# Lower parts of three slices and two weights moved behind the SSM mixer, and the last block's residual added by TensorE ahead of the mixer and at the end

## The chip, the cores and the metric

The program runs on one core of a Trainium2 chip. The core has a matrix engine (TensorE, PE in the profile), three engines for elementwise work (VectorE or DVE, ScalarE or ACT, GpSimd or POOL), and a queue engine (SyncE, SP) that does nothing here but issue transfers. Each engine runs its own instructions in a fixed order and waits for others by semaphores. The order is written into the program by a list scheduler that simulates the program beforehand; `self.order(x, y)` in the source only tells it to put x behind y. The metric is the device time of one execution in microseconds (us). Lower is better.

## What is computed

One inference step of a two-layer streaming encoder, for 1024 prompt positions and 64 sample positions with 1024 channels, in 32-bit floats. Layer 0 mixes tokens with banded attention, layer 1 with a complex diagonal state space model (S5). Around each mixer, and around the gated convolutional FFN behind it, stand two RMS norms and a residual:

```
h = x + rms_norm(mixer(rms_norm(x, g_pre_mix)),  g_post_mix)
x = h + rms_norm(conv_ffn(rms_norm(h, g_pre_ffn)), g_post_ffn)

rms_norm(x, g) = x * rsqrt(mean(x * x) + eps) * g

# mixer B, per group of 16 channels and complex state of 64
state[t] = lambda * state[t-1] + B u[t];   y = Re(C state) + D u
z = gelu(y);  ag = z @ w_glu + b_glu;  out = ag[:1024] * sigmoid(ag[1024:])

# conv_ffn
up = h @ w_up;  c = causal depthwise conv of width 3;  y = (gelu(c_a) * c_b) @ w_down
```

## The kernel before

**Layout.** Activations lie with channels on the 128 partitions: eight slices of 128 channels, and positions along the free axis. Positions are cut into three blocks of 384, 384 and 320 (blocks 0, 1 and 2; block 2 is "the last block" here). Two slices together are called a pair below, so a block has pairs 0 to 3.

**Products.** Large products are made from split operands. Each operand is the sum of an upper part, rounded to a format that TensorE takes at full rate (`h`, as in `zh`, `whl[:, 0]`), and a lower part, the rest (`l`). A product is three matmuls (`mm3`, L222): upper weight with lower activation, upper with upper, lower weight with upper activation. The upper part is copied by ScalarE and the lower part is a subtraction on VectorE. For weights this is `split_unit` (L214, timed at L217): a unit of 128x1024 is loaded into one of two `raw` buffers and split into `whl`. Plain 32-bit matmuls, as those with the identity, are made by TensorE in two recorded instructions each.

**From the first FFN to the mixer.** `ffn` ends with block 2's down projection (`down`, L637). `post_norm` (L312) then takes the statistics (`rstd`, L238: squares on ScalarE, sums on VectorE, a matmul with a column of ones at L267, a root at L271, three small VectorE operations, a transpose at L285 that brings the factor into PSUM as `pr`). In `apply`, VectorE multiplies each pair by `pr` (L329), and the residual `xs` (tiles `xl`, loaded long before) is added at L332. For block 2 behind the first FFN all four additions are VectorE's; at the program's end pairs 0 and 2 are GpSimd's and pairs 1 and 3 VectorE's, and each pair is stored at once (L336).

`ssm_norm` (L1154) takes the mixer's own statistics of the result. Meanwhile TensorE runs `fill` matmuls (L228, timed at L231), which compute nothing that is used: eight ahead of the statistics and one behind them. The factor goes through `ex` (L1181) and a matmul (L1182) into `rs` (L1184, L1185), by which the mixer's input is scaled. In parallel `ssm_bounce` (L1120) copies each pair into tiles `xs` in another order (L1140, ScalarE) and SP writes them to `hd` in DRAM (L1146); `ssm_load` (L1187) reads them back as `U` with channels and time rearranged, one quarter (two slices) at a time in two halves.

**The mixer** (`ssm`, L1205) runs 32 pairs of groups in batches of one or two. A batch loads its parameters (`pm`, five tiles ahead, L1222), multiplies into PSUM (L1258), and goes through VectorE: two products with cosine and sine tables (L1289, L1294), an addition (L1295, for which GpSimd puts in the initial state `h` at L1293), a scan (L1306), two products (L1309, L1310). TensorE then makes the output (L1318, L1324) and ScalarE copies it into `ys` (L1332). ScalarE also prepares `sc` (L1266) and `rd` (L1270) for each batch. After every four groups a slice is complete: it is written to `yd` (L1339), read back transposed as `yf` (L1344, on SP's queue), goes through the gelu into `z` (L1359), is copied into `zh` (L1368), and its lower part `zl` is subtracted on VectorE (L1372), which lies between the batches' own VectorE work. On the way the first two weights of the GLU are loaded and split (L1276, L217).

**The GLU** behind it (`tile_`, L1411) starts with output slice 0 of all three blocks, first with input slices 0 to 5, then 6, then 7, and goes on with products only. Beside it GpSimd and VectorE form sums of the second FFN's weights (L1391 to L1399).

**At the end** the second FFN's block 2 takes the same `post_norm`, and its stores end the program.

## Time and profile before

| what | value |
|---|---|
| median of three runs | 2239.77 us (2237.23 to 2244.5) |
| the profiled execution's own time | 2241.03 us |
| its span | 2239.2 us |
| TensorE busy | 2191.6 us, 98% of the span |
| VectorE busy | 1661.3 us, 74% |
| ScalarE busy | 1042.3 us, 47% |
| GpSimd busy | 412.8 us, 18% |
| mean granted TensorE clock | 0.992 of full |
| DMA, over the span | 428.47 MB, mean 191 GB/s |

The span runs from the first to the last instruction of the profiled execution. Times in the rows are us from its start. A row of a timeline gives start and duration, the engine, the line, the operation, what it writes and reads, a shape and a count of merged instructions; in brackets stands the idle time of the engine just before it and what ended it. A "q" behind the engine's name means its sequencer, which issues transfers. A DMA row in the chain of waits runs from issue to landing. A row of groups gives busy time and mean nanoseconds of one. A row of transfer issues gives a count, the size of each, and the median time from issue to landing.

### The profile page before, as it was taken

Reading aid. Unit: us, or ns where it says so; the run is one execution under the profiler, and the core shown is the slowest. Engines: PE = TensorE matmul, PEld = TensorE weight load, DVE = VectorE, ACT = ScalarE, POOL = GpSimd, SP = SyncE. Lnnn points to the kernel's source line nnn. Section 1 sums busy time; section 2 is a strip of 40 time slices with the busy share of each in tenths; the row PEclk is TensorE's granted clock in tenths of the full one; section 3 lists DMA queues with packets and bytes.
Section 4 is the critical chain, followed back from the end, with each engine's and each line's share of the span. In section 5 each row is a group of like instructions: output and inputs, shape, how many; then the busy total and the mean of one; then the engine's idle time right before and its main releaser. Section 6 shows DMA issues by size and latency. Waiting matters only on the chain.

```text
span 2239.2 us, 35982 instructions
## 1 busy us (share of the span) xinstructions
PE 2191.6 (98%) x13875; PEld 2117.1 (95%) x13875; DVE 1661.3 (74%) x2886; ACT 1042.3 (47%) x1890; POOL 412.8 (18%) x474
## 2 busy tenths in 40 slices
PE   9999999999999999999988899999999999999997
PEld 8987789999999999999986699999999999999997
DVE  8687647989878877767758855597976776676764
ACT  5255747422343342555545641263555455455543
POOL 5322004200032423000200034352010110110000
PEclk9999999999999999999999899999999999999999
DMA  5100015655355565887749888752266686579772
GB/s 197 37 22 29 20 62 158 241 188 202 122 150 173 176 208 187 274 279 236 233 163 339 263 280 294 249 167 75 87 224 229 218 297 226 196 272 314 218 253 97
DMA packets 208123, 428.47 MB, mean 191 GB/s; under 512 B 23312, under 2 KB 114224, under 8 KB 205008
## 3 DMA queue, kind: packets, MB, share of 16 engines
q1 hardware_dynamic: 175648, 326.56, 44.2%
q0 software_dynamic: 23984, 95.12, 11.9%
q10 hardware_dynamic: 8320, 4.49, 0.8%
q8 instruction: 109, 1.79, 0.3%
q14 instruction: 62, 0.51, 0.1%
HBM read 297.75 MB, written 128.37 MB: 190 GB/s over the span
## 4 chain that ended last, share of the span: by engine, by line
PE 32%; DMA 13%; DVE 9%; issue 4%; ACT 2%; POOL 2%; SPq 0%; DVEq 0%; ACTq 0%; POOLq 0%
PE mm L224 10%; PE mm L226 10%; PE mm L225 10%; DMA sj<-in_w_up 3%; DMA raw<-in_w_down 2%; DMA jw<-in_w_down 2%; DMA raw<-sd 1%; POOL sj L1391 1%; DMA yd<-ys 1%; DVE whl L217 1%; DMA su<-sj 1%; DMA gd<-t 1%; DVE gt L564 1%; DVE t L425 1%; DMA yf<-yd 1%
## 5 line engine op out<-in xcount | busy, mean ns | idle before, releaser
L224 PE MATMUL mm<-hl,whl 128*128 128x384 f32 (+1 forms) x1960 | 643.3, 329 | 4.1 <-DVE hl L307 3.1
L226 PE MATMUL mm<-hh,whl 128*128 128x384 f32 (+1 forms) x1960 | 641.2, 329 | 2.3 <-DVE whl L217 2.3
L225 PE MATMUL mm<-hh,whl 128*128 128x384 f32 (+1 forms) x1960 | 643.1, 328 | 0.0
L224 PEld LDWEIGHTS mm<-hl,whl 128*128 128x128 f32 x1960 | 368.4, 188 | 6.5 <-DVE hl L307 4.7
L226 PEld LDWEIGHTS mm<-hh,whl 128*128 128x128 f32 x1960 | 368.4, 188 | 3.0 <-DVE whl L217 2.9
L225 PEld LDWEIGHTS mm<-hh,whl 128*128 128x128 f32 x1960 | 368.6, 188 | 0.1
L217 DVE TENSOR_TENSOR whl<-raw,whl 128x1024 fp32r<-128x1024 f32 x202 | 254.9, 1263 | 146.7 <-ACT whl L217 146.2
L217 ACT ACTIVATE whl<-raw 128x1024 fp32r<-128x1024 f32 x202 | 213.0, 1058 | 248.1 <-PE mm L226 128.6
L224 PE MATMUL mm<-gt,whl 128*128 128x384 f32 (+1 forms) x968 | 316.8, 327 | 2.9 <-ACT whl L217 2.4
L226 PE MATMUL mm<-gt,whl 128*128 128x384 f32 (+1 forms) x968 | 315.8, 327 | 0.7 <-DVE whl L217 0.7
L225 PE MATMUL mm<-gt,whl 128*128 128x384 f32 (+1 forms) x968 | 315.9, 327 | 0.0
L224 PEld LDWEIGHTS mm<-gt,whl 128*128 128x128 f32 x968 | 181.7, 188 | 3.7 <-ACT whl L217 2.6
L226 PEld LDWEIGHTS mm<-gt,whl 128*128 128x128 f32 x968 | 181.7, 188 | 1.2 <-DVE whl L217 1.2
L225 PEld LDWEIGHTS mm<-gt,whl 128*128 128x128 f32 x968 | 181.8, 188 | 0.0
L195 DVE TENSOR_TENSOR whl<-raw,whl 128x1024 fp32r<-128x1024 f32 x84 | 96.4, 1154 | 72.7 <-ACT whl L194 71.3
L424 DVE SCALAR_TENSOR_TENSOR t<-u,ppt,t 128x1090 f32<-128x1090 f32 x88 | 126.9, 1443 | 5.8 <-ACT t L423 4.1
L194 ACT ACTIVATE whl<-raw 128x1024 fp32r<-128x1024 f32 x84 | 82.6, 987 | 101.8 <-DMA raw<-sd 40.1
L423 ACT ACTIVATE t<-u,ppt 128x1090 f32<-128x1090 f32 x88 | 114.2, 1298 | 26.2 <-DVE u L520 13.6
L425 DVE SCALAR_TENSOR_TENSOR t<-u,ppt,t 128x1090 f32<-128x1090 f32 x88 | 122.0, 1386 | 0.4
L415 DVE TENSOR_TENSOR u<-rb,mm 128x384 f32<-128x384 f32 (+1 forms) x164 | 80.8, 504 | 31.2 <-PE mm L226 26.4
L438 ACT ACTIVATE t<-t 128x1090 f32<-128x1090 f32 x44 | 49.1, 1115 | 113.1 <-DVE t L425 113.1
L564 DVE TENSOR_TENSOR gt<-gr,gt 128x768 fp32r<-128x768 f32 (+2 forms) x106 | 90.5, 881 | 11.1 <-ACT gt L563 10.2
(389 smaller groups left out, 4141.5 us busy)
## 6 DMA issues: line engine op xcount, KB each, us to landing
raw<-in_w_up SPq DMA_DIRECT2D x88, 512.0 KB, 4.4
raw<-in_w_down SPq DMA_DIRECT2D x74, 512.0 KB, 4.4
raw<-sd SPq DMA_DIRECT2D x40, 512.0 KB, 4.9
sj<-in_w_up POOLq DMA_DIRECT2D x68, 256.0 KB, 6.1
su<-sj POOLq DMA_DIRECT2D x34, 512.0 KB, 5.9
raw<-su SPq DMA_DIRECT2D x34, 512.0 KB, 4.6
pm<-prm SPq DMA_DIRECT2D x32, 522.0 KB, 8.2
gr<-td SPq DMA_DIRECT2D x40, 384.0 KB, 5.6
```

Source lines behind the costliest of these rows:

```text
L194: nc.scalar.activation(w[:, 0], raw, AF.Copy)
L195: nc.vector.tensor_sub(w[:, 1], raw, w[:, 0].bitcast(F32))
L217: x = nc.scalar.activation(w[:, 0], raw, AF.Copy), nc.vector.tensor_sub(w[:, 1], raw, w[:, 0].bitcast(F32))
L224: nc.tensor.matmul(out, w[:, 0, sl], xl, start=start, stop=False, skip_group_check=more)
L225: nc.tensor.matmul(out, w[:, 0, sl], xh, start=False, stop=False, skip_group_check=more)
L226: self.last_mm = nc.tensor.matmul(out, w[:, 1, sl], xh, start=False, stop=stop, skip_group_check=more)
L415: nc.vector.tensor_mul(u[:, t0 + 2:t0 + 2 + np_], rb[:, t0:t0 + np_], ps[:, :np_])
L423: nc.scalar.activation(t, u[:, 0:T + 2], AF.Identity, bias=cb(m), scale=cw(0, m))
L424: nc.vector.scalar_tensor_tensor(t, u[:, 1:T + 3], cw(1, m), t, op0=ALU.mult, op1=ALU.add)
L425: self.last_conv = nc.vector.scalar_tensor_tensor(t, u[:, 2:T + 4], cw(2, m), t, op0=ALU.mult, op1=ALU.add)
L438: nc.scalar.activation(ta, ta, AF.Gelu_apprx_tanh)
L564: nc.vector.tensor_sub(x[:, 1, u], raw, x[:, 0, u].bitcast(F32))
```

## The change

Two parts, and what they need.

**Lower parts behind the mixer.** The lower parts of slices 3, 4 and 5 (`LATE`) and of the two weights that are split inside the mixer are no longer made between the batches. They are held as closures and issued behind the last batch: first the two weights, the later one first, then the three slices block by block. So slice 3's `z` keeps its buffer until then, and slices 4 and 5 take theirs from the `prep2` pool, whose three tiles become one. The GLU's first tiles begin with the product that needs no lower part, for input slices 0 to 5 of all three blocks, and take the other two products after that.

**The residual on TensorE.** For block 2 behind the first FFN (post 3) and at the end (post 7), the residual of slices 0 to 5 (0 to 4 at the end) is put into PSUM by a matmul with the identity, ahead of the normalized value, in the gaps of the statistics; the normalized slice is added by a second matmul with the identity. Behind the first FFN, squares and the copy of slice 0 into `xs` read the sums from PSUM, and VectorE adds the residual to `y` itself later, in three places; pair 3 is added as before. At the end ScalarE copies the sums to `y`, VectorE adds slice 5 and pair 3, and GpSimd no longer takes part. Eight fills and one become six behind the last sum and two behind the statistics. Of `xs`, only slice 0 is copied before the statistics; the rest is ordered behind their root. `rd` of the first batches is ordered behind the copies of `rs`.

```diff
+LATE = (3, 4, 5)
...
     def split_unit(self, raw):
...
+        x = [nc.scalar.activation(w[:, 0], raw, AF.Copy)]
+        low = lambda: nc.vector.tensor_sub(w[:, 1], raw, w[:, 0].bitcast(F32))
+        if self.held is not None:
+            self.held.append(low)
+            return w
+        x.append(low())
...
     def rstd(..., fine=False, ads=()):
...
+            sq = self.n2(n, "sqb" if ads and q % 2 else tag)
+            if ads and q < 3:
+                for j in range(2):
+                    ahead = nc.scalar.activation(sq[:, j], ads[2 * q + j], AF.Square)
+                if q:
+                    adder.tensor_add(acc, acc, sq)
+                else:
+                    acc = sq
+                continue
...
     def post_norm(self, y, b, g, xsrc, root, roomy, out=None, by=None):
...
+        own = roomy and b == 2
+        ads = [self.mm_ps("ad")[:, :n] for _ in range(6 if out is None else 5)] if own else []
+
+        def residual(ks, first):
+            for k in ks:
+                self.order(nc.tensor.matmul(ads[k], self.ident, xs[k // 2][:, k % 2], start=True, stop=False), first)
+        if own:
+            residual(range(3), self.last_mm)
         pr, _ = self.rstd(y, n, "sqa", root, alt=b % 2 if roomy else None, fine=b == 2)
+        if own:
+            residual((3, 4), self.last_st)
+            residual(range(5, len(ads)), self.last_tr)
...
         def apply():
             last = None
+            if own:
+                for q in range(4):
+                    yq = y[:, 2 * q:2 * q + 2]
+                    V.tensor_mul(yq, yq, pr[:, None, :n].to_broadcast([P, 2, n]))
+                    for k in range(2 * q, min(2 * q + 2, len(ads))):
+                        self.last_ad = nc.tensor.matmul(ads[k], self.ident, y[:, k], start=False, stop=True)
+                        if out is not None:
+                            nc.scalar.activation(y[:, k], ads[k], AF.Copy)
+                    if q == 3:
+                        if len(ads) < 6:
+                            V.tensor_add(y[:, 5], y[:, 5], xs[2][:, 1])
+                        V.tensor_add(yq, yq, xs[q])
+                for q in range(4 if out is not None else 0):
+                    nc.sync.dma_start(out[:, 2 * q:2 * q + 2], y[:, 2 * q:2 * q + 2])
+                return ads, xs
...
+        self.p2 = self.prep2.tile([P, 3, 1024], F32, name="p2", tag="p2", bufs=1)
...
     def ssm_bounce(self, xt, b, qs=range(4), ahead=None):
+            k0, k1 = (0, 2) if q or b < 2 else (0, 1) if ahead is not None else (1, 2)
...
+                if ahead is None:
+                    self.order(x, self.last_root)
...
     def ssm_norm(self, xt, b, last=None):
+        ads, xs = last if b == 2 else ((), ())
+        ps, r = self.rstd(xt, n, "sqa" if b == 2 else "sqb", True, ..., ads=ads)
         if b == 2:
-            idle = self.mm_ps("idle")
-            self.fill(idle, 8, 512, self.last_tr)
+            idle = self.sm_ps("idle", 0)
+            self.fill(idle, 6, 512, self.last_ad)
+            xq = xt[:, 0:2]
+            self.order(nc.vector.tensor_add(xq, xq, xs[0]), self.last_add)
...
-        self.fill(idle, 1, 512, self.last_st)
+        self.fill(idle, 2, 512, self.last_st)
...
         self.fill(idle, 1, 256, x)
+        for q in (1, 2):
+            xq = xt[:, 2 * q:2 * q + 2]
+            self.order(nc.vector.tensor_add(xq, xq, xs[q]), e)
...
-                    if out[0]:
-                        self.order(x, out[0])
+                    self.order(x, out[0] or self.last_rs)
                 if qs[-1] == 31:
                     self.wsrc.pop(0)
+                    self.held = held
...
+                    self.held = None
...
-                    z = self.t4([P, T], "z")
+                    if kt == LATE[1]:
+                        z = self.prep2.tile([P, 2, T], F32, name="z", tag="p2", bufs=1)
+                        late[:] = [z[:, x] for x in range(2)]
+                    z = late[kt - LATE[1]] if kt in LATE[1:] else self.t4([P, T], "z")
...
+                    if kt in LATE:
+                        zs[kt] = z
+                        return
...
             self.behind = out[0], ends[-1]
+            for low in reversed(held):
+                self.order(low(), ends[-1])
+            for b in range(3):
+                for k, z in zs.items():
+                    self.order(lower(b, k, z), ends[-1])
...
+                def products(ks, of=(0, 1, 2)):
                     for ps, w in ((pb, ws[m][1]), (pa, ws[m][0])):
                         for k in ks:
+                            for j in of:
+                                e, x = ((0, zh), (1, zh), (0, zl))[j]
+                                nc.tensor.matmul(ps[:, :n], w[:, e, k * P:(k + 1) * P], x[b][:, k], ...)
...
                     k0 = KD - 2
-                    products(range(k0))
+                    products(range(k0), (0,))
+                    yield
+                    products(range(k0), (1, 2))
                     yield
...
-                        c.ssm_bounce(y, b, [0])
-                    c.ssm_norm(y, b)
+                        c.ssm_bounce(y, b, [0], ahead=last[0][0])
+                    c.ssm_norm(y, b, last)
                     if b == 2:
-                        c.ssm_bounce(y, b, range(1, 4), dict(c.sq))
+                        c.ssm_bounce(y, b, range(4))
```

56 lines of the change are left out of this document (29 added, 27 removed).

## The prediction

> **What bounds the kernel now.** I read the page first, then a table of stretches, then the timelines of the places that the diff touches.
>
> ```profile
> span 2239.2 us, 35982 instructions
> ...
> 1190.00:1245.00 55.00, 47.98 (x515) 38.68 (x514) 44.30 (x68) 23.82 (x66) 2.42 (x17) 0.96 1.07 350
> 1245.00:1292.00 47.00, 43.30 (x405) 34.84 (x400) 45.42 (x70) 34.30 (x92) 1.95 (x16) 0.85 0.78 244
> ...
> 1300.00:1420.00 120.00, 120.00 (x727) 120.00 (x726) 66.68 (x142) 28.70 (x39) 56.90 (x87) 1.00 0.87 300
> ```
>
> The rows of stretches give the length, then the busy time of PE, weight load, DVE, ACT and POOL, the granted clock, the DMA share and GB/s. Behind the mixer TensorE has no free moment (120.00 of 120.00), and what is gained there is gained only where it stands: at the hand-over from the first FFN to mixer B, in the mixer, and at the end. The mixer is two stages with different limits. To 1245 the DMA engines are full (1.07, 350 GB/s) while DVE works 44.30 of 55; from 1245 DVE works 45.42 of 47.
>
> ```profile
> 1219.25 14.41 DMA yd<-ys
> ...
> 1226.25 2.05 ACT L1359 ACTIVATE z<-yf 128x1024 f32<-128x1024 f32 x1 [4.28 <-DMA yf<-yd]
> ...
> 1242.19 2.04 ACT L1359 ACTIVATE z<-yf 128x1024 f32<-128x1024 f32 x1 [8.01 <-DMA yf<-yd]
> ...
> 1228.95 1.03 DVE L1372 TENSOR_TENSOR zl<-z,zh 128x384 fp32r<-128x384 f32 x2 [2.52 <-ACT zh L1368]
> ...
> 1244.88 1.03 DVE L1372 TENSOR_TENSOR zl<-z,zh 128x384 fp32r<-128x384 f32 x2 [4.47 <-ACT zh L1368]
> ```
>
> DVE's two long idle times of the first stage, 2.52 and 4.47 us, stand ahead of the lower parts of slices 0 and 1. These wait for the gelu, the gelu for the transfer into yf, and that stands in a backlog: the write of yd ahead of it took 14.41 us.
>
> **The hand-over.**
>
> ```profile
> 1172.21 0.80 PE L267 MATMUL pr<-ones,sqa 128*128 128x1 f32 x6 [1.70 <-DVE sqa L250]
> ...
> 1174.93 8.21 PE L231 MATMUL idle<-ppt,ident 128*128 128x512 f32 x16
> ...
> 1179.54 1.88 PE L231 MATMUL idle<-ppt,ident 128*128 128x512 f32 x4
> ...
> 1185.34 0.83 PE L267 MATMUL pr<-ones,sqa 128*128 128x1 f32 x6 [2.20 <-DVE sqa L261]
> ...
> 1187.73 1.46 PE L1182 MATMUL pr<-sel 128*128 128x16 f32 x6 [0.60 <-DVE sel L1181]
> ...
> 1175.17 0.82 DVE L329 TENSOR_TENSOR y<-y,pr 128x640 f32<-128x640 f32 x1 [0.99 <-PE pr L285]
> ...
> L249 ACT ACTIVATE sqa<-y 128x320 f32<-128x320 f32 x2 | 0.9, 462 | 2.6 <-DVE y L658 2.6
> ...
> 1187.86 1.77 ACT L1270 ACTIVATE rd<-mask,rho 128x276 f32<-128x276 f32 x4 [1.39 <-POOL mask L1245]
> ...
> 1186.84 0.57 POOL L1239 DMA_DIRECT2D h<-in_s_h  x1 [55.56 <-ACT nvsqa L271]
> ...
> 1192.82 0.19 POOL L1293 COPY wk<-h 128x2 f32<-128x2 f32 x1 [4.99 <-DMA h<-in_s_h]
> ```
>
> No identity matmul of 320 columns stands in the trace. The nearest is a fill of 512, two records. Two of them lie in 1.88 us: at most 0.94 each, some 0.86 from start to start, as the records overlap; with part of it at half clock, 8.21 / 8 = 1.03. By columns I take 0.55 for 320, bounds 0.5 and 1.03. The three ahead of the first statistics (1.65) fit their gap of 1.70, and the other three come behind L267 and L285, where TensorE waits for DVE too: cost nothing, and 0.5 if the gap is overrun.
>
> Before, DVE multiplies and adds by turns from 1175.17, and the second statistics start at 1185.34. After: the first product to 1175.99, six sums on TensorE to 1179.3, the square of the last slice 0.46, two additions of a pair at 0.82 (the product's shape), a half one of 0.5 (384 columns take 0.53 in a row below): 1181.9, 3.4 earlier. TensorE takes most of that back. Between the last sum and L1182 stand six and two fills (8 x 0.86 = 6.9) and 0.83 of statistics, so L1182 starts at 1179.3 + 7.7 = 1187.0, against 1187.73. The copies of sel behind it gain 0.44 more, as rd no longer holds ScalarE until 1189.63 (L1182 ends at 1189.19); rd now waits for them, and the scans that read it come later. The load of h is released by the second root, and the first addition of the mixer waits for h (1192.82). The root is 3 earlier if the statistics come between the fills, 1 if all six stand ahead. For the compute side I take 2.8, bounds 1.0 and 3.4. The three additions that are moved (0.82 each) lie in DVE's waits for the root and for L1182. The sums hold the six mm banks, which the mixer wants only behind the squares; the merged prep2 tile belongs to a side job of the first FFN: nothing for both.
>
> The queue speaks against it. Only slice 0 goes to hd early. Slice 1, pair 1 and pair 2, which today go out while the residual is still being added, now wait for the second root, and pairs 1 and 2 for additions behind L1181 as well. SP issues in order: behind those writes stand the reads of U and then the pm loads.
>
> ```profile
> hd<-xs SPq DMA_DIRECT2D x2, 548.0 KB, 3.3
> ...
> 1179.00:1181.00 2.00, 2.00 (x6) 0.93 (x5) 1.97 (x4) 1.66 (x3) 0.00 (x0) 1.00 0.96 397
> 1181.00:1183.00 2.00, 2.00 (x5) 0.59 (x4) 1.94 (x3) 0.74 (x1) 0.00 (x0) 1.00 0.78 197
> 1183.00:1185.00 2.00, 0.13 (x1) 0.00 (x0) 1.16 (x3) 1.84 (x4) 0.00 (x0) 1.00 0.96 268
> 1185.00:1187.00 2.00, 1.66 (x8) 0.97 (x8) 0.71 (x5) 1.47 (x4) 0.16 (x1) 1.00 1.04 425
> ```
>
> Before, 2 x (397 + 197 + 268) = 1724 KB move from 1179 to 1185, and 850 more to 1187. After, until the root frees the rest, only one slice and U's first half can move, 2 x 548 KB. With an early root some 630 KB are missing at 1185, with a late one 1480 at 1187. At 350 GB/s that is 1.8 and 4.2 us, by which all that follows in the full queue is later. So the shift at the end of the second stall lies between -2.8 (compute decides) and +4.2 (the queue, late root). I take the middle, +0.7: the earlier writes of yd pull one way, the late restart the other.
>
> **The mixer's second stage.**
>
> ```profile
> 1267.63 1.02 DVE L1372 TENSOR_TENSOR zl<-z,zh 128x384 fp32r<-128x384 f32 x2
> ...
> 1269.79 0.47 DVE L1372 TENSOR_TENSOR zl<-z,zh 128x320 fp32r<-128x320 f32 x1
> ...
> 1278.74 1.22 DVE L217 TENSOR_TENSOR whl<-raw,whl 128x1024 fp32r<-128x1024 f32 x1
> ...
> 1281.09 1.40 DVE L1372 TENSOR_TENSOR zl<-z,zh 128x384 fp32r<-128x384 f32 x3
> ...
> 1284.52 1.22 DVE L217 TENSOR_TENSOR whl<-raw,whl 128x1024 fp32r<-128x1024 f32 x1
> ...
> 1289.83 0.53 DVE L1372 TENSOR_TENSOR zl<-z,zh 128x384 fp32r<-128x384 f32 x1
> ...
> 1290.63 0.95 DVE L1372 TENSOR_TENSOR zl<-z,zh 128x384 fp32r<-128x384 f32 x2
> 1291.51 0.44 DVE L1310 TENSOR_TENSOR wk<-wk,sc 128x276 f32<-128x276 f32 x1
> ...
> 1283.29 2.42 PE L1324 MATMUL p<-wk,pm 64*128 64x137 f32 x16 [2.06 <-DVE wk L1309]
> ...
> 1292.69 1.20 PE L1324 MATMUL p<-wk,pm 64*128 64x137 f32 x16
> ...
> 1294.44 0.44 PE L224 MATMUL pb<-zl,whl 128*128 128x384 f32 x1 [0.55 <-ACT ys L1332]
> ...
> 1281.00:1285.00 4.00, 1.94 (x14) 1.57 (x14) 3.96 (x9) 4.00 (x8) 0.22 (x2) 0.76 0.93 252
> ```
>
> The lower parts of slices 3, 4 and 5 and of two weights take 1.02 + 0.47 + 1.22 + 1.40 + 1.22 + 0.53 + 0.95 = 6.8, less 0.07 of overlap at each of seven pieces (1290.63 + 0.95 against 1291.51): 6.3 us, out of a stretch in which DVE hardly waits. While DVE did them TensorE stood 2.06 and came back at half speed (2.42 against 1.20). Its last group ends at 1293.89, 0.7 later than DVE's last product at 1291.95 and 1.20 behind it. Half of the 0.7 I count, since TensorE has less room beside a quicker DVE: 6.6, bounds 7.0 and 4.1. The lower bound is ScalarE, busy 4.00 of 4.00 in the last row: if its chain moves by slice 3's 1.4 alone, 2.5 of the 3.9 us saved until 1284 become waits.
>
> Behind the mixer the 6.3 us cost nothing. DVE is free 2.5 us ahead of the GLU, which now begins with 36 products of upper parts, 5.9 us at 120 / 727 = 0.165. The second weight's lower part is first in the new order (1.22) and wanted after those; block 0's three slices follow. Without the cover TensorE would stand 6.3 - 2.5 = 3.8. The held weights keep both raw buffers longer, so SP's next weight load waits, and behind it slice 7's yf, which waits for its yd anyway; the next weights are wanted after 144 products, 23.8 us into the GLU.
>
> **The end.**
>
> ```profile
> 2229.29 1.55 DVE L329 TENSOR_TENSOR y<-y,pr 128x640 f32<-128x640 f32 x2 [0.90 <-PE pr L285]
> ...
> 2233.95 1.58 DVE L332 TENSOR_TENSOR y<-y,xl 128x640 f32<-128x640 f32 x1
> ...
> 2231.80 4.18 SPq L336 DMA_DIRECT2D out_o_y<-y  x4
> ...
> 2230.00:2232.00 2.00, 0.00 (x0) 0.00 (x0) 1.97 (x3) 0.00 (x0) 1.53 (x1) 0.50 0.00 0
> ```
>
> Before, the last addition ends at 2235.53 and SP's last issue at 2235.98. After, four products end at 2232.4, a half addition and one of a pair (0.82, no GpSimd beside it) at 2233.7. TensorE's five sums run from 2230.1 to 2232.9, and the copy out ends at 2233.4. The last issue then ends near 2234.2, 1.75 earlier. At half clock the sums take 1.1 each, the copy ends at 2236.1, and the last issue, two stores on, at 2236.8: 0.85 later.
>
> That last row grants 0.50 to an idle TensorE. [...]
>
> **Sum.** +0.7 - 6.6 - 1.75 = -7.65. The profiled run's span of 2239.2 becomes 2231.55; that run took 2241.03, which becomes 2233.4. The median of the runs shown is 2239.77, 1.26 below it, so 2232.1.
>
> **Rivals.** (1) Compute decides the first stage too: -2.8 for +0.7, 2228.6. For it: yd is issued earlier and so stands further ahead in the backlog; against it: a DMA share of 1.07. (2) All six fills stand ahead of the statistics and the root comes late: +4.2, 2235.6. For it: fills wait for nothing else. (3) The lower parts are moved but weren't the limit, ScalarE was: 4.1 for 6.6, 2234.6; against it, DVE hardly waits there. (4) Half clock at the end, +0.85 for -1.75: 2234.7; against it, the gaps now hold five matmuls, 2.75 us. (5) Slower: the late restart lengthens both stalls, TensorE stands longer in each and comes back at half clock as at 1283.29. A group of 16 then costs 1.2 more, and a spell of two and a half groups 3. With 4.2, the two additions behind L1181 (1.6) and two spells (6), 11.8 - 8.35 = 3.45 slower, 2243.2; it decides from 8.35 us of delay on.
>
> **Chances.** Forecast 0.42, (1) 0.17, (2) 0.17, (3) 0.10, (4) 0.08, (5) 0.06. A measurement of this kernel tells about 0.3%, 6.7 us, from no change, so faster means under 2233.05. The forecast, uncertain by 1.7 of its own, gives 0.31 of that, (1) 0.17, the others 0.07: faster 0.55, same 0.39, slower 0.06. Range 2227.0 to 2237.5, which leaves (5) and the ends of the others out; the forecast alone 2230 to 2234.
>
> **What would show it.** Right: no L217 and no zl on DVE between slice 2 and the last scan; the GLU's first matmul some 6 us earlier; DVE's idle time ahead of zl of slices 0 and 1 grown from 7 to 8 or more in sum; TensorE at full clock from 1267 on; the last store less than 10 us behind the last FFN matmul. Wrong: DVE waiting for ScalarE or TensorE in the second stage; a first stage that begins 3 us earlier and ends 3 us earlier; a root behind 1185.

## The result, and the profile after

The changed kernel takes 2249.94 us, the median of six executions (2245.86 to 2255.89), beside 2239.88 us for the kernel before (six, 2237.23 to 2244.5). The ratio is 1.0052, with a 95% interval of 1.0037 to 1.0067: 10 us slower by the medians, where 2232.1 and a range of 2227.0 to 2237.5 were forecast. The profiled execution of after took 2254.37 us, with a span of 2252.6 us and a mean granted clock of 0.989, against 0.992 before. It is the second slowest of the six and has the lowest clock of them (the others 0.991 to 0.993), so what its profile shows of the clock is likely more than the median execution has.

I cut both traces at the same events. T0 is the end of the first FFN's last matmul, M0 the mixer's first matmul, S2 the start of slice 2's first lower part, V the end of VectorE's last product in the mixer, G0 the GLU's first matmul, F the last FFN's last matmul.

| stretch, us | before | after | difference |
|---|---|---|---|
| start to T0 (hardly changed there) | 1170.5 | 1172.2 | +1.6 |
| T0 to M0, the hand-over | 19.8 | 18.0 | -1.8 |
| M0 to S2, the mixer's first stage | 66.0 | 80.3 | +14.3 |
| S2 to V, its second stage | 35.7 | 30.6 | -5.1 |
| V to G0 | 2.5 | 2.3 | -0.2 |
| G0 to F, GLU and second FFN | 930.3 | 935.9 | +5.6 |
| F to the end of the last store's issue | 11.25 | 9.60 | -1.65 |
| behind that | 3.2 | 3.8 | +0.6 |

The rows sum to 13.4, as the spans differ by 2252.6 - 2239.2 = 13.4. The first row differs by more between kernels that are the same up to there: T0 lies at 1167.0 to 1170.9 in before, e3, e5 and e13 below, and at 1167.0 to 1174.4 over all profiles. Two stretches lose, the first stage and the GLU. The second stage and the end win what was forecast, or nearly.

**The first stage.** The table of stretches of after, columns as in the prediction:

```profile
1190.00:1245.00 55.00, 48.30 (x346) 38.28 (x346) 34.10 (x53) 20.18 (x53) 2.05 (x13) 0.75 0.92 304
1245.00:1292.00 47.00, 44.34 (x485) 35.52 (x486) 42.16 (x59) 34.46 (x93) 2.15 (x17) 1.00 0.94 281
...
1205.00:1215.00 10.00, 8.00 (x39) 6.18 (x39) 4.76 (x7) 3.04 (x9) 0.19 (x1) 0.61 1.04 391
1215.00:1225.00 10.00, 10.00 (x47) 8.03 (x47) 5.16 (x7) 0.40 (x1) 0.30 (x2) 0.50 0.96 318
1225.00:1235.00 10.00, 10.00 (x48) 7.62 (x46) 4.86 (x6) 2.37 (x8) 0.30 (x2) 0.52 0.69 200
1235.00:1245.00 10.00, 10.00 (x117) 8.35 (x116) 7.78 (x12) 6.98 (x14) 0.49 (x3) 1.00 0.94 285
```

From 1190 to 1245 the granted clock is 0.75 where it was 0.96, and VectorE works 34.10 us of 55 where it worked 44.30. From inside the row that begins at 1205 (0.61) to 1235 TensorE runs at half speed, by the records without a pause (10.00 of 10.00 from 1215 on), and VectorE has half its time free. Such a run of half clock is called a spell below; this one lasts 27.3 us. VectorE's timeline, and TensorE's, both of after:

```profile
1197.51 0.50 DVE L1256 TENSOR_TENSOR U<-U,sel 128x328 f32<-128x328 f32 x1 [2.24 <-DMA U<-hd]
...
1218.75 0.72 DVE L1343 TENSOR_TENSOR wk<-pm,p 128x548 f32<-128x548 f32 x1 [8.88 <-PE p L238]
...
1226.81 0.72 DVE L1343 TENSOR_TENSOR wk<-pm,p 128x548 f32<-128x548 f32 x1 [2.73 <-PE p L238]
...
1235.12 0.72 DVE L1343 TENSOR_TENSOR wk<-pm,p 128x548 f32<-128x548 f32 x1 [3.23 <-PE p L238]
...
1244.38 1.03 DVE L1440 TENSOR_TENSOR zl<-z,zh 128x384 fp32r<-128x384 f32 x2 [1.76 <-ACT zh L1425]
...
1257.15 1.03 DVE L1440 TENSOR_TENSOR zl<-z,zh 128x384 fp32r<-128x384 f32 x2 [1.31 <-ACT zh L1425]
```

```profile
1223.59 2.10 PE L1311 MATMUL p<-U,pm 128*64 128x137 f32 x16
...
1231.70 2.09 PE L1311 MATMUL p<-U,pm 128*64 128x137 f32 x16
...
1242.98 1.16 PE L1311 MATMUL p<-U,pm 128*64 128x137 f32 x16
...
1248.07 1.16 PE L1311 MATMUL p<-U,pm 128*64 128x137 f32 x16
```

The input matmuls of a batch of two groups come every 1231.70 - 1223.59 = 8.1 us at half clock, and every 1248.07 - 1242.98 = 5.1 at full clock. So while the spell lasts TensorE is the bound of the stage, and VectorE waits 8.88, 2.73 and 3.23 us for its products. Its waits ahead of the lower parts of slices 0 and 1, by contrast, fell to 1.76 and 1.31; the likely reason is that VectorE itself is so late that the transfers are in time.

**The GLU** starts at 1303.31 instead of 1294.44. Then, on TensorE and on SP's queue, after first and before second:

```profile
1282.19 0.91 SPq L210 DMA_DIRECT2D raw<-in_w_glu  x2
...
1302.26 6.77 SPq L210 DMA_DIRECT2D raw<-in_w_glu  x3
...
1459.72 1.34 PE L285 MATMUL pr<-ones,sqa 128*128 128x1 f32 x6 [2.69 <-DVE sqa L279]
```

```profile
1268.56 0.91 SPq L209 DMA_DIRECT2D raw<-in_w_glu  x2
...
1279.98 6.12 SPq L209 DMA_DIRECT2D raw<-in_w_glu  x2
...
1446.14 0.83 PE L267 MATMUL pr<-ones,sqa 128*128 128x1 f32 x6 [0.29 <-DVE sqa L261]
```

Before, two further units of the GLU's weights are loaded at 1279.98, inside the mixer. After, three are issued from 1302.26 on, as the GLU begins. The first statistics behind the GLU come 1446.14 - 1294.44 = 151.7 us behind its start before, and 156.4 after; TensorE stands 2.69 us ahead of them and takes them at a lower speed (1.34 against 0.83).

### The profile page after: what moved, and what is told of

Read it like the earlier page. It is cut to its first block, busy times and chain, and to the rows that moved or that the text cites. A ratio compares the mean times of both kernels' runs of the same rounds, so it can differ in the third digit from the quotient of the medians.

```text
span 2252.6 us, 36091 instructions
## 1 busy us (share of the span) xinstructions
PE 2215.6 (98%) x13917; PEld 2136.9 (95%) x13917; DVE 1661.1 (74%) x2886; ACT 1045.1 (46%) x1900; POOL 411.4 (18%) x472
## 4 chain that ended last, share of the span: by engine, by line
PE 73%; DMA 11%; DVE 9%; issue 3%; ACT 2%; POOL 1%; SPq 0%; POOLq 0%; DVEq 0%; ACTq 0%
PE mm L231 19%; PE mm L233 19%; PE mm L232 19%; DMA raw<-in_w_down 3%; DMA sj<-in_w_up 3%; PE po L847 2%; PE tps L840 1%; PE sps L817 1%; DMA raw<-sd 1%; DVE whl L220 1%; PE p L1378 1%; DMA su<-sj 1%; PE gq L231 1%; PE pb L1497 1%; PE pa L1497 1%
## 5 line engine op out<-in xcount | busy, mean ns | idle before, releaser
L220 DVE TENSOR_TENSOR whl<-raw,whl 128x1024 fp32r<-128x1024 f32 x202 | 256.1, 1270 | 155.6 <-ACT whl L219 154.9
```

The source lines that it names most:

```text
L220: low = lambda: nc.vector.tensor_sub(w[:, 1], raw, w[:, 0].bitcast(F32))
```

## The experiments

Eighteen kernels, each measured against the kernel before on the same chip. M0-S2, spell (the longest run of half clock that reaches into M0 to S2; in e10 and e13 it begins 1.3 and 4.2 us ahead of M0), S2-V, G0-stat (G0 to the first statistics behind the GLU), G0-F and T0-G0 are from the one profiled execution of each, in us; the ratio is from all its executions.

| kernel | ratio, 95% interval | T0-G0 | M0-S2 | spell | S2-V | G0-stat | G0-F |
|---|---|---|---|---|---|---|---|
| before | 1 | 123.9 | 66.0 | 6.8 | 35.7 | 151.7 | 930.3 |
| after | 1.0052, 1.0037-1.0067 | 131.2 | 80.3 | 27.3 | 30.6 | 156.4 | 935.9 |
| e1 lower parts alone | 1.0005, 0.9992-1.0018 | 116.8 | 64.6 | 6.8 | 30.6 | 153.5 | 931.4 |
| e2 hand-over alone | 1.0072, 1.0060-1.0085 | 138.9 | 79.1 | 30.7 | 39.6 | 151.2 | 928.2 |
| e3 end alone | 1.0007, 0.9998-1.0016 | 122.1 | 65.3 | 6.8 | 35.7 | 151.3 | 928.2 |
| e4 = e1 + e3 | 1.0004, 0.9990-1.0019 | 118.2 | 64.2 | 6.8 | 31.1 | 152.1 | 928.5 |
| e5 before, late writes | 1.0025, 1.0012-1.0038 | 127.9 | 69.3 | 6.8 | 35.8 | 152.7 | 929.0 |
| e6 after, early writes | 1.0015, 0.9999-1.0030 | 117.0 | 65.8 | 3.4 | 30.8 | 157.1 | 936.6 |
| e7 e4, yd first | 1.0020, 1.0007-1.0034 | 117.3 | 64.8 | 6.8 | 30.6 | 156.2 | 935.0 |
| e8 e6, yd first | 1.0013, 0.9997-1.0029 | 117.2 | 66.0 | 3.4 | 30.7 | 154.3 | 930.7 |
| e9 e4, only slices held | 0.9985, 0.9972-0.9997 | 119.0 | 65.0 | 6.8 | 32.5 | 151.6 | 930.2 |
| e10 e1, only weights held | 1.0021, 1.0005-1.0037 | 119.2 | 64.5 | 6.8 | 33.8 | 157.7 | 938.8 |
| e11 e6, only slices held | 1.0004, 0.9988-1.0020 | 131.3 | 73.7 | 17.1 | 36.3 | 151.3 | 928.1 |
| e12 after, pair 1 first | 1.0074, 1.0056-1.0092 | 140.3 | 82.0 | 30.7 | 33.7 | 152.6 | 931.0 |
| e13 e5, pair 1 last | 1.0041, 1.0021-1.0060 | 128.9 | 68.5 | 10.2 | 37.3 | 152.2 | 931.5 |
| e14 after, 10 fills, 3 batches | 1.0063, 1.0044-1.0081 | 129.2 | 78.5 | 3.4 | 30.6 | 158.3 | 939.6 |
| e15 after, 10 fills, 1 batch | 1.0059, 1.0036-1.0082 | 124.6 | 73.8 | none | 30.8 | 157.1 | 938.1 |
| e16 after, 3 fills, 8 batches | 1.0064, 1.0046-1.0083 | 130.1 | 76.9 | 17.1 | 32.6 | 157.8 | 937.7 |
| e17 e2, 4 fills, 1 batch | 1.0049, 1.0031-1.0067 | 126.5 | 71.4 | 6.8 | 35.7 | 151.3 | 927.3 |
| e18 e2, 10 fills, 1 batch | 1.0025, 1.0012-1.0039 | 127.6 | 72.4 | 3.4 | 35.8 | 151.3 | 927.5 |

One profile is one execution. T0 moves by some 7 us and executions of one kernel differ by up to 20, so the stretches tell where time went and the ratios tell how much.

### Each part alone: e1 to e4

e1 has the `LATE`, `held`, `lower` and `products` lines of the diff alone, e2 those of `rstd`, `post_norm` behind the first FFN, `ssm_bounce` and `ssm_norm`, e3 those of `post_norm` at the end, e4 is e1 with e3:

```diff
-        own = roomy and b == 2
+        own = roomy and b == 2 and out is None       # e2
+        own = roomy and b == 2 and out is not None   # e3, e4
```

> The kernel before with the lower parts alone moved behind the mixer (slices 3, 4 and 5, two weights, the GLU's new first step); the residual stays on VectorE and GpSimd. In the changed kernel the stretch from slice 2's lower part to the last product fell from 35.7 to 30.6 us, and the stretch from the GLU's first matmul to the last FFN matmul grew by 5.2. Theory A (the hand-over alone made the kernel slower; the lower parts do what was predicted): 5.1 to 6.6 us faster, 2233 to 2235. Theory B (the lower parts carry a price of their own: the two held weights keep both raw buffers, ScalarE's copies of the next two weights wait for their loads, and the last write of yd, the gelu of slice 6 and GpSimd's load of sj stand behind them in order): the last write of yd starts some 4 us after the GLU's first matmul instead of beside it, the first load of sj more than 9 us after it instead of 6, TensorE waits at the GLU's end; 0 to 2 us faster, 2238 to 2240. Theory C (the moved work was covered anyway): no change, and no shorter second stage.

> The kernel before with TensorE's residual at the hand-over alone, the writes of hd behind the second root with it. Theory A (the late restart of the SP queue starves the mixer's first stage, TensorE stands and falls to half clock): the stretch from the mixer's first matmul to the lower part of slice 2 grows by 10 us or more, as in the changed kernel (14.2), with a half-clock spell of over 15 us behind 1205; since the moved lower parts give nothing back here, 10 to 15 us slower, 2250 to 2255. Rival (the delay is the predicted 4.2 us and the long half-clock spell of the changed kernel's profile was a chance of that run): 2 to 5 us slower, 2242 to 2245, no spell of over 10 us. Rival (compute decides the first stage): 3 us faster, 2237.

> The kernel before with TensorE's residual at the end alone. In the changed kernel the last store's issue ends 9.8 us behind the last FFN matmul's start, before 11.0: 1.2 us faster, 2238.6, within what the measurement tells from no change. If the end's matmuls ran at half clock it would be 0.85 slower.

> The changed kernel with the hand-over of before: lower parts moved and TensorE's residual at the end, the first FFN's last block added by VectorE and written to hd as before. Theory A: 2231.5 to 2234, faster than both kernels. Theory B: 2236 to 2239. If the spell at half clock is not the hand-over's, TensorE at half clock for over 15 us behind 1205 here too, and 2245 or more.

e2 alone is slower than the whole change, 1.0072, and e1 and e3 are not slower than before, so the loss is the hand-over's. Its M0-S2 is 79.1 with a spell of 30.7, as in after. e1 gives the second stage its 5.1 (30.6 against 35.7) and yet no gain in the whole time. e3 shortens the end by 1.65, and its whole time doesn't show it (1.0007). The parts don't add up: +0.0072 + 0.0005 + 0.0007 = +0.0084, against +0.0052. Part of that is e2's second stage, which had a spell of its own: its row from 1292 to 1300 has a clock of 0.50, and S2-V is 39.6.

### The order of the writes: e5, e6

e5 gives the kernel before only the late writes: everything but slice 0 is copied behind the statistics' root. e6 takes them out of after: all pairs are added and copied ahead of the root.

```diff
 # e5, on before
-                    self.order(x, after[(0, 1, 3, 3)[q]])
+                    self.order(x, self.last_root)
...
+                    if after is not None:
+                        self.order(self.hw[q], self.last_root)
 # e6, on after
-                    self.order(x, self.last_root)
+                    self.order(x, self.sq[3])
...
-            xq = xt[:, 0:2]
-            self.order(nc.vector.tensor_add(xq, xq, xs[0]), self.last_add)
+            for q in range(3):
+                xq = xt[:, 2 * q:2 * q + 2]
+                self.order(nc.vector.tensor_add(xq, xq, xs[q]), self.last_add)
```

> The kernel before, residual on VectorE and GpSimd, lower parts where they were; only the copies and writes to hd of slice 1 and of pairs 1 to 3 wait for the second root, as the change makes them do. Theory A (the late writes of hd are the cause, above all that of pair 1, which the read of U(1) waits for; nothing of TensorE's residual is needed for it): the first read of U(1) starts 4 us or more later than before, the stretch from the mixer's first matmul to the lower part of slice 2 grows from 65 to 70 or more, and the kernel is 5 to 12 us slower (2241 to 2248), less than with the whole hand-over (15.7), since pair 1 here stands ahead of pairs 2 and 3 and waits for no addition. Rival (the delay comes from what the residual on TensorE does to the mixer's start, not from the queue): no change, and 65 us.

> The changed kernel with one thing undone: the additions of y for pairs 0 to 2 stand right behind the last addition of the statistics, and the copies into xs behind the last square instead of behind the root, so that the writes of hd need not wait for the root; TensorE's residual stays. Theory A: pair 1 is written at about 3.5 us behind the last sum's copy instead of 9, the read of U(1) comes 7 us or more earlier, the stretch from the mixer's first matmul to slice 2's lower part falls from 80 to 68 or less, no half-clock spell of over 10 us: 2233 to 2240, 10 us or more faster than the changed kernel. Rival (TensorE's residual itself, its fills or its cold start cause it): 76 or more of the 80 stay, and 2247 or more.

Late writes alone give a ratio of 1.0025, 5.6 us. They lengthen M0-S2 to 69.3, 3.3 more than in before and 4.0 more than in e3, whose writes are early too, and T0-M0 to 21.1. With early writes after's first stage is as short as before (65.8), its spell 3.4, and its ratio falls from 1.0052 to 1.0015. What reaches the queue, in SP's timelines of after, e5 and e6:

```profile
1179.15 0.32 SPq L1193 DMA_DIRECT2D hd<-xs  x1
...
1187.72 1.56 SPq L1193 DMA_DIRECT2D hd<-xs  x2
...
1191.54 2.30 SPq L1193 DMA_DIRECT2D hd<-xs  x2
...
1200.29 0.98 SPq L1248 DMA_DIRECT2D U<-hd  x2
1201.37 3.01 SPq L1275 DMA_DIRECT2D pm<-prm  x3
```

```profile
1178.72 8.96 SPq L1147 DMA_DIRECT2D hd<-xs  x3
1188.29 1.41 SPq L1147 DMA_DIRECT2D hd<-xs  x1
1189.79 5.65 SPq L1198 DMA_DIRECT2D U<-hd  x2
1195.55 6.69 SPq L1225 DMA_DIRECT2D pm<-prm  x6
```

```profile
1182.17 3.61 SPq L1193 DMA_DIRECT2D hd<-xs  x3
...
1192.14 2.13 SPq L1246 DMA_DIRECT2D U<-hd  x2
```

In after the second quarter of U is read at 1200.29, 10.1 us behind M0, in e6 at 1192.14, 2.9 behind M0, and the parameters behind it wait with it. But e5 reads it at 1189.79, 0.5 behind M0, pays 3.3 to 4.0 and gets no long spell. So the late writes explain some 4 of after's 14.3 by themselves, and the spell is the first candidate for the rest; what the late writes have to do with the spell is the next question.

### Is it pair 1's place in the queue: e12, e13

In after pair 1 is written behind pair 3, and U's second quarter needs pair 1. e12 puts it right behind slice 1 in after, e13 puts it last in e5.

```diff
 # e12, on after
+        before = self.last_root if b == 2 and ahead is None else None
...
-                    self.order(x, self.last_root)
+                    self.order(x, before)
+                    before = x
 # and the additions of pairs 0 to 2 behind self.last_add, as in e6
 # e13, on e5: the same chain of copies, and
-                        c.ssm_bounce(y, b, range(4), dict(c.sq))
+                        c.ssm_bounce(y, b, (0, 3, 2, 1), dict(c.sq))
```

> The changed kernel, with all writes of hd behind the root as the change has them, but in the order slice 1, pair 1, pair 2, pair 3, and with the additions for pairs 0 to 2 right behind the statistics, so that pair 1 is not last but one and waits for no addition. Late writes alone, in that order, on the kernel before cost 4 us of the stretch from the mixer's first matmul to slice 2's lower part (65.3 to 69.3). Theory A2 (10 of the 14.3 us come from pair 1's place: its write lands at 1200 and the read of U(1) waits for it; that wait is long enough for the long half-clock spell): the read of U(1) starts some 6 us earlier than in the changed kernel, the stretch is 68 to 72, no half-clock spell of over 10 us in it; 2238 to 2243. Rival (any write behind the root on top of TensorE's residual costs the whole): 77 or more and a spell of over 15 us, 2247 or more.

> The kernel before with the late writes of hd and nothing else, as in the run with late writes alone, but pair 1 written last instead of first. Theory A2: the read of U(1) waits for a write that lands at 1200 or later, the stretch from the mixer's first matmul to slice 2's lower part grows from 69 to 74 or more, 8 to 16 us slower than before. Rival: as with pair 1 first, 69 and 5 to 6 us slower.

Pair 1 first does what was meant, the second quarter of U is read 3.6 us behind M0 in place of 10.1, but it doesn't help: e12 is at 1.0074 with M0-S2 of 82.0 and a spell of 30.7. Pair 1 last brings no long spell: M0-S2 is 68.5 and the spell 10.2. My theory that the place of pair 1 makes the loss falls. e13's 1.0041 is more than e5's 1.0025, though the intervals overlap.

### Is it the clock itself: e14 to e18

These leave the order of the transfers alone and add `fill` matmuls of 238 columns in the first batches, which keep TensorE busy while it waits for U. Ten of them take 4.28 us in e14's trace, 0.43 each; the expectations of e14 and e16 put one at half of that.

```diff
-                    f = self.fill(p1s[-1][:, 0, 2 * NC_:], 1, 512 - 2 * NC_, x) if i == 0 else None
+                    f = self.fill(p1s[-1][:, 0, 2 * NC_:], 10 if 0 < qs[0] < 6 else 1, 512 - 2 * NC_, x) if i == 0 else None    # e14
+                    ... 10 if qs[0] == 1 else 1 ...        # e15, on after; e18, on e2
+                    ... 3 if 0 < qs[0] < 16 else 1 ...     # e16
+                    ... 4 if qs[0] == 1 else 1 ...         # e17, on e2
```

> The changed kernel with ten fill matmuls instead of one in the mixer's batches of pairs 1 to 4 (each some 0.2 us), so that TensorE has work while it waits for U(1) and pm; the writes of hd stay late. If the long half-clock spell is what makes 4 us of delay into 14: no spell of over 10 us, the stretch from the mixer's first matmul to slice 2's lower part falls from 80 to 70 to 74, 2240 to 2245. If the spell only fills time in which TensorE would have waited for data anyway: 78 or more.

> The changed kernel with ten fills instead of one in the mixer's batch of pair 1 alone (4.3 us of TensorE at a place where VectorE waited for none of it in the run with fills in three batches). That run had no half-clock spell, but VectorE waited 8.3 and 2.6 us behind the fills of its other two batches. Theory A3 (the late writes make TensorE stand, and the long half-clock spell that follows makes the 14 us: a batch of two pairs costs TensorE 5.1 us at full clock and VectorE 5.2, so that a spell of 27 us costs half its length): without the spell the stretch from the mixer's first matmul to slice 2's lower part is 68 to 73, 2240 to 2245, 7 us or more faster than the changed kernel. Rival (the spell fills time in which data would be missing anyway): 77 or more without a spell.

> The changed kernel with three fills instead of one in each of the mixer's batches of pairs 1 to 15 (0.43 us more a batch, some 3.5 us in all where TensorE or VectorE waits for them). Theory A3: TensorE stands less between 1195 and 1210; where the spell stays away or ends within 10 us, the stretch is 69 to 75, 2241 to 2247. If spells come and last as before (over 20 us), fills of this number neither keep TensorE's clock nor bring it back, and the stretch is 82 or more.

> The kernel before with TensorE's residual at the hand-over alone (1.0072 times the time of before; 79.1 us from the mixer's first matmul to slice 2's lower part, a spell of 30.7 us at half clock), and four fills instead of one in the batch of pair 1. They take 1.7 us, of TensorE's time that it otherwise stands in behind that batch. Theory A3 (the spell makes 6 to 9 of the 14 us, late data the rest): without a long spell the stretch is 70 to 73 and the ratio 1.0033 to 1.0045. With a spell of over 15 us: 76 or more and 1.006 or more.

> The same with ten fills there (4.3 us, of which some 2.4 lie behind the next batch's work). On the whole changed kernel these took the spell away and brought the stretch to 73.75, but its GLU hid the gain in the whole time. Theory A3: no long spell, 72 to 74.5, ratio 1.004 to 1.0055. Rival (the spell fills time in which data would be missing anyway): 77 or more, and a ratio of 1.0065 or more.

The pair to look at is e2 and e18, which differ by nine fills. The tables of stretches, e2 first, then e18:

```profile
1205.00:1215.00 10.00, 10.00 (x42) 7.43 (x42) 1.12 (x3) 2.65 (x9) 0.03 (x1) 0.50 1.01 391
1215.00:1225.00 10.00, 10.00 (x44) 7.79 (x42) 6.97 (x10) 0.40 (x1) 0.46 (x3) 0.50 0.92 248
```

```profile
1205.00:1215.00 10.00, 10.00 (x72) 7.86 (x71) 4.78 (x7) 3.31 (x11) 0.19 (x1) 1.00 1.04 398
1215.00:1225.00 10.00, 10.00 (x101) 8.09 (x100) 9.62 (x14) 2.77 (x9) 0.59 (x4) 1.00 1.04 305
```

Clock 0.50 against 1.00, VectorE 1.12 + 6.97 = 8.1 us against 14.4, and the ratio falls from 1.0072 to 1.0025, by 0.0047 or 10.5 us. The data are as late in both: SP reads the second quarter of U at 1195.74 in e2 and at 1198.23 in e18, 10.1 us behind M0 each time. Nor is the clock that of one lucky profile: the mean granted clock lies at 0.987 to 0.991 in all six executions of e2, and at 0.993 to 0.998 in all twelve of e18 (0.989 to 0.993 in the six of after). By the two profiles 6.7 of the gain lie in the first stage (79.1 to 72.4) and 3.8 in the second, where e2 has a further spell of 10.2 us and e18 one of 3.4. An estimate from the batches is of the same size for after: its spell, 27.3 us, holds 27.3 / 8.1 = 3.4 batches, each 8.1 - 5.1 = 3.0 us too long, 10.1 us in all. What is left in e18, 1.0025, is as much as e5 pays for late writes alone.

The other four are less clean, and none of the three on the changed kernel itself is faster than it. e14 has no long spell and yet 78.5, as its rival forecast; here the fills sit ahead of the products that VectorE waits for.

```profile
1217.24 0.72 DVE L1343 TENSOR_TENSOR wk<-pm,p 128x548 f32<-128x548 f32 x1 [8.27 <-PE p L238]
```

e15, with fills in one batch, has no spell and 73.8, but its whole time is not better than after's (1.0059, its interval from 1.0036). Its profile gains 6.5 us to G0 and gives back 2.2 in the GLU and 1.9 behind the issue of the last store; the late GLU, below, is only part of the reason. After's profile also has more half clock than its other executions: an estimate from the mean clocks, twice what is missing to 1, gives some 40 us of half clock in 2248 at 0.991, where the profile has 51. So the share of the spell in the median execution of the changed kernel is less than the profile's, and stays open. e16's few fills shorten the spell to 17.1 only. e17's profile, with a spell of 6.8, was the fastest of its six executions (2241.83, mean clock 0.995; the others 2244.09 to 2251.91 at 0.990 to 0.993), so its 71.4 is not typical of its ratio of 1.0049. What four fills do is not settled.

### Why the gain of the second stage doesn't arrive: e7 to e11

In e1 and e4 the mixer ends 5.7 to 7.1 us earlier (T0-G0) and the whole time is as before. Two theories for the GLU. One: VectorE and the write of `yd` come late behind the held lower parts, and with them the sums of the second FFN's weights (`sj`). e7 and e8 order them first. Two: the held weights keep both `raw` buffers, and the next loads move into the GLU. e9 and e11 hold the slices only, e10 the weights only.

```diff
 # e7 on e4, e8 on e6
-            self.behind = out[0], ends[-1]
+            self.behind = out[-1], ends[-1]
 # and the addition into fo ahead of the held slices
 # e9 on e4, e11 on e6
-                    self.held = held
-                    self.held = None
 # e10, on e1
-LATE = (3, 4, 5)
+LATE = (-1, -1, -1)
```

> The kernel with lower parts moved and TensorE's residual at the end, hand-over as before, and two things moved at the GLU's start: ScalarE's copies of the next two weights come behind the last write of yd, and the addition into fo stands ahead of the held slices on VectorE. Theory B (the moved lower parts gain 5 us in the mixer and lose it on average in the GLU, through the late start of the loads of sj): the last write of yd starts beside the GLU's first matmul, the first load of sj 6 us behind it instead of 10, TensorE waits for nothing at the GLU's end, and 2228 to 2231, 5 us faster than the kernel before. Theory C (the loss sits elsewhere): no change, 2234 to 2237, as with the lower parts and the end alone.

> The early writes of hd and the moved yd and fo together, on the changed kernel. If A and B hold both: as the one without the hand-over, 2228 to 2232. If A alone: 2233 to 2238. If neither: 2247 or more.

> Lower parts of slices 3 to 5 behind the mixer and TensorE's residual at the end, hand-over as before; the lower parts of the two weights stay in the mixer, so that the raw buffers come free there. In all profiles so far in which the weights were held, the loads of the third and fourth weight land 2.4 to 6.6 us behind the GLU's first matmul, otherwise 4 to 10 us ahead of it, and the chain of sj and su ends 152 to 157 us behind it, where TensorE wants its result at 151. Theory D (two loads of 512 KB each pushed from the mixer into the GLU, whose transfers are full, delay that chain; TensorE waits for its end and falls to half clock): the loads land ahead of the GLU's first matmul again, the last write of su lands by 152, TensorE waits less than 1 us there; the second stage is some 3.5 us shorter than before, the end 1.65: 2231 to 2233, about 5 us faster than the kernel before. Rival (the slices' lower parts on VectorE at the GLU's start delay the chain): it still ends at 154 or later, and no change.

> The kernel before with the lower parts of the two weights alone held until behind the mixer (and the GLU's new first step); slices 3 to 5 stay in it. Theory D: the loads of the third and fourth weight land 2 us or more behind the GLU's first matmul, the last write of su lands at 154 to 157, TensorE waits 2 to 5 us there; what the mixer gains (1 to 2.3) is lost, 2237 to 2241. Rival (the slices delay the chain, not the weights): the chain ends by 152, and 1 to 2 us faster, 2235.

> The changed kernel with the early writes of hd and the weights' lower parts back in the mixer. If A and D hold: from the first FFN's last matmul to the mixer's slice 2 84 us as with the early writes, second stage 3.5 us shorter than before, the chain of su ends by 152, the end 1.65 shorter: 2229 to 2232, 5 to 7 us faster than the kernel before. If D falls: 2236 to 2241.

The first theory falls: e7's loads of `sj` begin 4.0 us behind G0 in place of e4's 9.9, and yet its statistics come 156.2 us behind G0, no earlier. In e8 they come 2.8 us earlier than in e6, and the ratio stays (1.0013 and 1.0015). The second is borne out by e9 and e10. SP's queue and TensorE of e9, then of e10:

```profile
1279.37 5.47 SPq L210 DMA_DIRECT2D raw<-in_w_glu  x2
...
1442.94 0.83 PE L274 MATMUL pr<-ones,sqa 128*128 128x1 f32 x6
```

```profile
1290.89 6.13 SPq L210 DMA_DIRECT2D raw<-in_w_glu  x3
...
1448.92 1.44 PE L274 MATMUL pr<-ones,sqa 128*128 128x1 f32 x6 [4.99 <-DVE sqa L268]
```

e9's GLU begins at 1291.39, and its loads go out 12 us before that (14.5 in the kernel before); TensorE takes the statistics without a wait, 151.6 us behind G0. e10's GLU begins at 1291.25, three loads go out as it begins, TensorE waits 4.99 us and the statistics come at 157.7. The price goes on behind the wait. In the ten profiles of changed kernels with statistics at 151.2 to 152.7, G0-F is 927.3 to 931.5; in the seven at 156.2 and more it is 935.0 to 939.6, and each of these seven has a half-clock spell of 6.8 or 10.2 us at the statistics, where the ten have none but e12's of 3.4. That the two loads crowd out the chain's own transfers is argued, not shown: the GLU's DMA share is high but not full (in after 0.85 from 1300 to 1420, at 289 GB/s).

Holding the weights doesn't always cost. e4 and e12 hold them too, the first of the loads goes out 2.3 and 3.8 us ahead of G0, and the statistics come at 152.1 and 152.6. In the seven late ones it goes out 1.4 us ahead or less, but so it does in e1 and e8, with statistics at 153.5 and 154.3. And e4's profiled execution, 2229.43, was the second fastest of its twelve (median 2235.69), so it isn't typical either.

e9 is the one kernel whose interval lies below 1: 0.9985, 0.9972 to 0.9997, 3.3 us by the medians (2236.63 against 2239.94). It is the best of eighteen with its upper end close to 1, so it should be measured again before it is believed. e11 adds e6's hand-over to it, was expected 5 to 7 us faster than the kernel before, and is at 1.0004. Its profile, the slowest of its twelve executions, has a spell of 17.1 in the first stage although its writes are early and U is read 3.1 us behind M0. So long spells don't need late writes.

## Why the prediction was wrong, by its steps

**The hand-over: "+0.7", between "-2.8" and "+4.2". This is the step that failed.** Its parts on the engines were right. The matmul put at 1187.0 starts at 1188.40, or 1186.8 when T0's 1.64 is taken off. Rival (2) took place: all six fills lie ahead of the statistics, and the root comes behind 1185, at 1186.77 (1185.1 without the 1.64), where this was named as a sign against the forecast.

```profile
1180.86 5.31 PE L238 MATMUL idle<-ppt,ident 128*128 128x512 f32 x12
...
1186.01 0.72 PE L285 MATMUL pr<-ones,sqa 128*128 128x1 f32 x6
...
1186.77 0.26 ACT L289 ACTIVATE nvsqa<-pr,eps 128x3 f32<-128x3 f32 x1 [4.65 <-PE pr L285]
...
1188.40 0.75 PE L1232 MATMUL pr<-sel 128*128 128x16 f32 x6
```

Six fills leave 12 records, ended by 1186.17, and the statistics follow. The queue's price of 4.2 for a late root is close to what e5 measures in the first stage, 3.3 to 4.0. What the step lacked is the clock. I had bounded the delay as a shift, by which everything "is later", and had half clock in rival (5) only, as two spells of 3 us with a chance of 0.06. Half clock behind a late restart, as in (5), is what the profiles show, but as one spell of 27 to 31 us whose price is some 7 us by e2 and e18 and 10 by the estimate, and it came without longer stalls: the two waits ahead of slices 0 and 1, which (5) has lengthened, fell from 7.0 to 3.1 us in sum. Measured in the profile the step was -1.8 + 14.3 = +12.5 in place of +0.7. Why the spell sets in and lasts stays open.

**The second stage: "-6.6, bounds 7.0 and 4.1". Right within its bounds**, -5.1. The clock is full from 1245 to 1292 (1.00 against 0.85), and no `zl` and no L220 stands between slice 2 and the last product; they come behind it, in VectorE's timeline of after:

```profile
1270.44 1.03 DVE L1440 TENSOR_TENSOR zl<-z,zh 128x384 fp32r<-128x384 f32 x2 [1.83 <-ACT zh L1425]
...
1300.61 0.45 DVE L1364 TENSOR_TENSOR wk<-wk,sc 128x276 f32<-128x276 f32 x1
1300.97 2.35 DVE L220 TENSOR_TENSOR whl<-raw,whl 128x1024 fp32r<-128x1024 f32 x2
1303.24 4.10 DVE L1440 TENSOR_TENSOR zl<-z,zh 128x384 fp32r<-128x384 f32 x9
```

The slices alone give 3.2 (e9), the weights alone 1.9 (e10). What is missing to 6.6 is mostly size: VectorE's work between slice 2 and its last product fell by 5.6 us (34.54 to 28.95), not 6.3, and its idle time rose by 0.5.

**"Behind the mixer the 6.3 us cost nothing." Wrong by 5.6 us in after's profile.** VectorE's work was covered, as I had it: lower parts from 1300.97 to 1307.34, under 36 products. But I had seen that "The held weights keep both raw buffers longer", and asked only when their weights are wanted, 23.8 us into the GLU. The question was also what their transfers collide with, in a stage in which the DMA share was 0.87 before.

**The end: "-1.75". Right in the trace**, -1.65, with no half clock (1.00 from 2239 to 2251 in after): 9.60 or 9.61 us from the last FFN matmul to the end of the last store's issue in every kernel that has this part. That e3's whole time doesn't gain (0.9998 to 1.0016) stays open; its profiled execution shows nothing that is longer.

**The sign that failed first** was the one I gave as "DVE's idle time ahead of zl of slices 0 and 1 grown from 7 to 8 or more in sum". It fell to 3.1, while VectorE waits ahead of that for TensorE. I had named DVE and DMA as the first stage's limits and not asked how far TensorE, with 47.98 of 55 us busy at a clock of 0.96, was from becoming one: at half clock, with 8.1 us a batch in place of 5.1, it is.

## What to carry to other kernels

Where TensorE is busy for most of a stage that something else bounds, ask what the stage costs at half clock, batch by batch (here 8.1 us in place of 5.1); a delay at its entry may not be a shift but a change of clock (here 0.50 for 27.3 us of after's profile). When work is put behind a stage, ask not only whether the engine has room there but which buffers it holds, which loads wait for these, and whether their queue has room where they now fall. Parts that are measured one by one need not add up: the part that gained in its stage was hidden here by a side effect of its own, and by e9 half of it alone was worth more than the whole. And read a profile beside the times of the other executions: after's, e4's, e11's and e17's were each near an end of theirs.

## What the runs showed of the hardware

Runs of half clock between M0 and S2 come in lengths of 3.4, 6.8, 10.2, 17.1, 27.3 and 30.7 us, all multiples of 3.41 in these profiles. By the records TensorE is busy for 10.00 of 10.00 us from 1215 to 1225 in after and from 1205 to 1225 in e2, and the granted clock stays at 0.50; these spells last 27.3 and 30.7 us. In the 14 us ahead of the spells of after, e2 and e12 TensorE's longest idle time is 2.5, 2.4 and 1.8 us. With ten fills in one batch the profiles show no long spell (none in e15, 3.4 us in e18). What starts and ends a long spell is open: e5, with late writes, had none, and e11, with early ones, had one of 17.1. With early writes a spell of 6.8 us left no trace in the first stage's length: before, e1, e3, e4, e7 and e9 have one and an M0-S2 of 64.2 to 66.0; e6 and e8, with 3.4, have 65.8 and 66.0.

The records of 32-bit matmuls are no count of the work in these stretches. In TensorE's timeline of after the same line leaves sixteen records at 1200.27 and eight at 1206.05, in the same time and at full clock:

```profile
1200.27 1.20 PE L1378 MATMUL p<-wk,pm 64*128 64x137 f32 x16
...
1206.05 1.20 PE L1378 MATMUL p<-wk,pm 64*128 64x137 f32 x8
...
1218.59 2.19 PE L1378 MATMUL p<-wk,pm 64*128 64x137 f32 x8
```

The third row is the group of eight records at half clock, 2.19 us. The counts per 10 us above (47, 48, 117) can't be compared for that reason.
